# First layer's cross attention: query products of two heads from seven block products each, woven with keys and values in a written order; raw weights in five 4 KB tiles

## The chip, the cores and the metric

The kernel runs on one core of a Trainium2 chip. That core has a matrix engine (PE, with its weight loads shown apart as PEld), a vector engine (DVE), a scalar engine (ACT), GpSimd (POOL) and a queue engine (SP) which issues transfers; each works through its own instructions in the order in which they were recorded, and semaphores tie the engines together. The metric is the device time of one execution in microseconds (us); lower is better.

## What is computed

A trunk of two decoder layers over 512 tokens of width 1024, in float32. Each layer runs a SwiGLU block, a token mixer, a cross attention into 256 memory tokens and a second SwiGLU block, and each step ends in a layer norm of the scaled residual sum. The change concerns the cross attention of layer 0 alone:

```python
def memory_cross_attention(x, mem, wq, wkv, wo):
    B, S, _ = x.shape
    M = mem.shape[1]
    q = (x @ wq).reshape(B, S, XA_HEADS, XA_HEAD_DIM)
    k, v = jnp.split(mem @ wkv, 2, axis=-1)
...
    s = jnp.einsum('bshd,bmhd->bhsm', q, k).astype(jnp.float32) * (XA_HEAD_DIM ** -0.5)
    p = jax.nn.softmax(s, axis=-1).astype(v.dtype)
    o = jnp.einsum('bhsm,bmhd->bshd', p, v).reshape(B, S, D_MODEL)
    return o @ wo
...
        x = layer_norm(a * x + memory_cross_attention(x, mem, xa_wq[i], xa_wkv[i], xa_wo[i]),
                       ln_g[i, 2], ln_b[i, 2])
```

There are 4 heads of width 256; x is 512x1024, wq 1024x1024, wkv 1024x2048.

## The kernel before

Every float32 operand of a matmul is kept as two fp32r parts, a high part (a cast on ACT, L120) and a low part (the difference, on DVE, L121). `mm3` (L205 to L207) forms one product from three matmuls: high by high, low by high, high by low. A weight block of 128x1024 elements is therefore loaded into a tile `raw`, cast on ACT into `wh` and subtracted on DVE into `wl` before PE can use it; there are five buffers each of `wh` and `wl` here, and two of `raw` (8 KB a partition, 1 MB a transfer).

The cross attention of layer 0 follows the differential attention. Its last output product ends in a layer norm for each of the four groups of 128 tokens, `X0` to `X3`: `ln_token` (L366 to L380) on DVE, ACT and POOL, then eight transposes on PE (L489) and four halves of a split, which give the transposed input `xh`, `xl`. Tokens 2 and 3 come late, and `turn_late` puts their transposes behind the first products with the memory, which need no x.

`xa_main` then goes head by head: keys (`xa_k`, result `pk`), values (`xa_v`, `pv`), queries (`xq`). For the queries of a head it takes two blocks of 128 columns of wq, and for each eight `mm3` over 512 tokens. Beside it, `xa_side` yields the heads' attention in six pieces each (scores `xs`, softmax `mx`, `p`, `rx`, transposes `pt`, values `xo`), and `weave` hands out one such piece for every 2500 ns of matmul time that it counts for the main line. `to_tokens` multiplies the outputs `oT` of the first two heads by `xa_wo` while the last heads finish; a second call does the rest and ends in the layer norm of the next step.

The SwiGLU blocks already use seven block products in place of eight (`up`, L681 ff., with `second_factors`, L611 to L644, for the sums of blocks of x). There `more` (L666) adds a further block of weights onto a raw tile in memory by an accumulating transfer, which POOL issues.

The recorded order on an engine is made by a scheduler from the order of the program and its own model of time; the transfers of a queue run in the order in which they were issued.

## Time and profile before

| what | us |
|---|---|
| median of 3 runs | 1932.35 (1931.14 to 1932.38) |
| the profiled execution, its time | 1930.48 |
| the profiled execution, its span | 1928.7 |
| PE busy in it | 1900.9 |
| DVE busy in it | 1564.0 |
| ACT busy in it | 1021.8 |
| POOL busy in it | 315.3 |

The span runs from the first to the last instruction. All times below that begin at some point "of the span" are microseconds from its start. Instructions on one engine overlap a little, so that the distance from start to start is shorter than the duration in a row: two 128x1024 differences that follow each other take 2.35 us, one 1.22 us. The cross attention of layer 0 lies between about 588 and 744 us.

### The profile page before, as it was taken

How to read it: one execution, taken by the hardware profiler on the slowest of the kernel's cores; microseconds unless marked ns; L12 is line 12 of the kernel's file. 1: busy time of each engine (PE TensorE's matmuls, PEld its weight loads, DVE VectorE, ACT ScalarE, POOL GpSimd, SP SyncE). 2: the span in 40 equal slices, each digit the busy share in tenths (PEclk: the TensorE clock that was granted, in tenths of full speed). 3: DMA queues.
4: the chain of work that ended last, by engine and by line, in shares of the span. 5: the costliest groups of instructions: out<-in, count | busy, mean ns of one | idle time of the engine just before them, and what ended most of it. 6: DMA issues, size and time to landing. Idle time of an engine off the chain costs nothing.

```text
span 1928.7 us, 32510 instructions
## 1 busy us (share of the span) xinstructions
PE 1900.9 (99%) x13114; PEld 1740.4 (90%) x13114; DVE 1564.0 (81%) x2200; ACT 1021.8 (53%) x1580; POOL 315.3 (16%) x276
## 2 busy tenths in 40 slices
PE   8999999999999999999999999999999999999998
PEld 8999998888878888999998999999889889999997
DVE  7888889888867558889888988898887568998886
ACT  6555454567755435645554655455445436555553
POOL 2112121111210001211220311212040012111210
PEclk9999999999999999999999999999999999999999
DMA  9978772322124317987785587878244356877861
GB/s 241 217 167 186 169 145 77 91 66 88 64 90 153 110 66 190 182 178 162 144 192 178 106 179 164 181 165 183 85 153 142 110 138 120 180 158 170 183 133 57
DMA packets 246743, 277.96 MB, mean 144 GB/s; under 512 B 8256, under 2 KB 212544, under 8 KB 246592
## 3 DMA queue, kind: packets, MB, share of 16 engines
q0 software_dynamic: 92928, 92.29, 31.3%
q1 hardware_dynamic: 153664, 183.59, 29.7%
q8 instruction: 103, 1.69, 0.4%
q14 instruction: 48, 0.39, 0.1%
HBM read 273.75 MB, written 2.10 MB: 143 GB/s over the span
## 4 chain that ended last, share of the span: by engine, by line
PE 77%; DVE 13%; ACT 3%; DMA 3%; issue 2%; POOL 1%; SPq 1%; DVEq 0%; POOLq 0%; ACTq 0%
PE x L205 6%; PE x L206 6%; PE x L207 6%; PE z L206 4%; PE z L205 4%; PE z L207 4%; PE ps L205 4%; PE ps L207 4%; PE ps L206 4%; DVE wl L121 3%; DMA ra<-in_ffn_w_in_dram 2%; PE px L207 2%; PE px L205 2%; PE px L206 2%; PE y L207 2%
## 5 line engine op out<-in xcount | busy, mean ns | idle before, releaser
L666 POOL DMA_DIRECT2D ra<-in_ffn_w_in_dram x132 | 170.3, 1310 | 990.7 <-DVE wl L121 955.0
L120 ACT CAST wh<-ra 128x1024 fp32r<-128x1024 f32 x184 | 193.7, 1053 | 218.0 <-PE x L206 69.1
L121 DVE TENSOR_TENSOR wl<-ra,wh 128x1024 fp32r<-128x1024 f32 x184 | 223.8, 1220 | 72.0 <-ACT wh L120 71.5
L120 ACT CAST wh<-rc 128x1024 fp32r<-128x1024 f32 x136 | 143.1, 1053 | 118.8 <-PE x L206 43.1
L205 PE MATMUL x<-xe,wh 128*128 128x256 f32 x704 | 195.0, 277 | 0.0
L206 PE MATMUL x<-xe,wh 128*128 128x256 f32 x704 | 194.8, 277 | 0.0
L207 PE MATMUL x<-xe,wl 128*128 128x256 f32 x704 | 194.8, 277 | 0.0
L121 DVE TENSOR_TENSOR wl<-rc,wh 128x1024 fp32r<-128x1024 f32 x136 | 164.7, 1219 | 28.2 <-ACT wh L120 27.9
L120 ACT CAST wh<-b 128x1024 fp32r<-128x1024 f32 x112 | 117.8, 1052 | 131.7 <-PE x L206 67.8
L121 DVE TENSOR_TENSOR wl<-b,wh 128x1024 fp32r<-128x1024 f32 x112 | 136.7, 1221 | 40.2 <-ACT wh L120 40.2
L205 PE MATMUL x<-xh,wh 128*128 128x256 f32 x544 | 151.1, 278 | 0.0
L206 PE MATMUL x<-xl,wh 128*128 128x256 f32 x544 | 150.6, 277 | 0.0
L207 PE MATMUL x<-xh,wl 128*128 128x256 f32 x544 | 150.6, 277 | 0.0
L206 PEld LDWEIGHTS x<-xe,wh 128*128 128x128 f32 x704 | 132.5, 188 | 1.4
L205 PEld LDWEIGHTS x<-xe,wh 128*128 128x128 f32 x704 | 132.1, 188 | 1.3
L207 PEld LDWEIGHTS x<-xe,wl 128*128 128x128 f32 x704 | 132.2, 188 | 0.0
L121 DVE TENSOR_TENSOR wl<-raw,wh 128x1024 fp32r<-128x1024 f32 x64 | 80.3, 1259 | 39.6 <-ACT wh L120 39.1
L206 PEld LDWEIGHTS x<-xl,wh 128*128 128x128 f32 x544 | 102.5, 188 | 0.7
L205 PEld LDWEIGHTS x<-xh,wh 128*128 128x128 f32 x544 | 102.1, 188 | 0.7
L207 PEld LDWEIGHTS x<-xh,wl 128*128 128x128 f32 x544 | 102.2, 188 | 0.0
L207 PE MATMUL y<-xh,wl 128*128 128x256 f32 x352 | 98.6, 280 | 2.1 <-DVE wl L121 0.9
L205 PE MATMUL z<-xh,wh 128*128 128x256 f32 x352 | 97.5, 277 | 0.7 <-ACT xh L120 0.7
(429 smaller groups left out, 6288.9 us busy)
## 6 DMA issues: line engine op xcount, KB each, us to landing
ra<-in_ffn_w_in_dram POOLq DMA_DIRECT2D x132, 512.0 KB, 6.8
rc<-in_ffn_w_in_dram SPq DMA_DIRECT2D x88, 512.0 KB, 5.8
b<-in_ffn_w_out_dram SPq DMA_DIRECT2D x76, 512.0 KB, 4.9
ra<-in_ffn_w_in_dram SPq DMA_DIRECT2D x44, 512.0 KB, 5.3
rc<-in_ffn_w_in_dram POOLq DMA_DIRECT2D x44, 512.0 KB, 7.4
raw<-in_xa_wkv_dram SPq DMA_DIRECT2D x16, 1024.0 KB, 5.5
raw<-in_da_w_qkv_dram SPq DMA_DIRECT2D x16, 512.0 KB, 5.2
raw<-in_xa_wq_dram SPq DMA_DIRECT2D x8, 1024.0 KB, 5.1
```

Of the source, the lines that this page charges most:

```text
L120: self.nc.scalar.copy(hi, src),
L121: self.nc.vector.tensor_sub(lo, src, hi.bitcast(F32)),
L205: mm(out, w[0], x[0], start=start, stop=False, skip_group_check=again)
L206: mm(out, w[0], x[1], start=False, stop=False, skip_group_check=again)
L207: self.last_mm = mm(out, w[1], x[0], start=False, stop=stop, skip_group_check=again)
L666: nc.gpsimd.dma_start(t, source(*block), accum_op=ALU.add)
```

## The change

In layer 0 the queries of heads 0 and 1 (work `a`) and of heads 2 and 3 (work `b`) are each one product of a 512x1024 x with a 1024x512 block of wq, cut into 2x2 blocks and formed from seven block products instead of eight (`query_parts`): 24 matmuls of 256 columns each. The weight operands of products 3, 4 and 2 come from the same raw tile `ra` by accumulating transfers (`more`), each behind the split before it; products 6 and 5 use `rd` in the same way. The blocks of x and their sums (`xa_factors`) take the place of the plain transposed x of tokens 2 and 3. Keys and values are cut into quarters of 512 KB, and one list, `XA_ORDER`, sets the order in which pieces of all these works are recorded. There are now four buffers of `wh` and `wl`, and five raw tiles of 4 KB.

```diff
+XA_ORDER = (
+    "k0 k0 k0 v0 s v0 v0 k1 k1 k1 s v1 v1 v1 "
+    "a a k2 a k2 a v2 a v2 a a A "
+    "b b k2 b b k3 v2 b b k3 b B k3 v3 v3 v3"
+)
...
-        self.ln_next_gb, self.kv_bufs = None, 8
+        self.ln_next_gb, self.kv_bufs, self.raw_rows = None, 8, 4
...
-        got = []
-        for k in range(0, kn, 4):
-            n = min(4, kn - k)
-            raw = self.raw_tile((4, S))
+        got, n = [], self.raw_rows
+        for k in range(0, kn, n):
+            raw = self.raw_tile((n, S))
...
+        self.by_factors = self.ln_next == "ffn" or self.ln_next == "xa" and layer == 0
...
-            o = self.pair("oT")
+            if layer:
+                o = self.pair("oT")
+            else:
+                if c == 0:
+                    both = self.pair("oT" if len(self.oT) < 4 else "xe", (P, 2, S))
+                o = both[0][:, c], both[1][:, c]
             self.split(o[0], o[1], po)
             self.oT.append(o)
...
+    def key_parts(self, w, h, turn=iter(())):
+        ps = self.mm("pk").rearrange("p (c n) -> p c n", c=2)
+        for j in range(2):
+            wk = self.hl([P, KC, P])
+            self.split_weights(wk[0], wk[1], self.raw_quarter(w, 0, h * 256 + j * P, P))
+            for k in range(KC):
+                yield self.mm3(
+                    ps[:, j], (wk[0][:, k], wk[1][:, k]), self.memT[k], k == 0, k == KC - 1
+                )
+            yield None
+        few(turn, 1)
+        kt = self.kv_tiles((P, 2, MEM))
+        self.split(kt[0], kt[1], ps)
+        self.kts.append(kt)
+        yield None
+    def value_parts(self, w, h):
+        ps = self.mm("pv").rearrange("p (m n) -> p m n", m=2)
+        for half in range(2):
+            wv = self.hl([P, 4, MEM])
+            self.split_weights(wv[0], wv[1], self.raw_quarter(w, half * S, D + h * 256, 256))
+            for m in range(2):
+                o = slice(m * P, (m + 1) * P)
+                for k in range(4):
+                    mt = self.memT[half * 4 + k]
+                    yield self.mm3(
+                        ps[:, m], (mt[0][:, o], mt[1][:, o]), (wv[0][:, k], wv[1][:, k]),
+                        half == m == k == 0, half == m == 1 and k == 3, True,
+                    )
+            yield None
+        v = self.kv_tiles((P, 2, MEM))
+        self.split(v[0], v[1], ps)
+        self.kv.append((self.kts[h], v))
+        yield None
+    def xa_factors(self):
+        nc, F, H = self.nc, self.factors, 2 * P
+        a11, a12, a21, s1 = (self.tmp("oT", (P, 4, H)) for i in range(4))
+        def part(i, x, o=slice(0, H)):
+            self.split(F[i][0][:, :, o], F[i][1][:, :, o], x)
+        for t in (2, 3):
+            o = slice(t % 2 * P, (t % 2 + 1) * P)
+            pts = []
+            for half in range(2):
+                pt = self.aux("pt", ("py", "yz")[half]).rearrange("p (c n) -> p c n", c=4)
+                c0 = half * S
+                with self.behind():
+                    self.transpose4(pt, [self.X[t][:, c0 + j * P : c0 + (j + 1) * P] for j in range(4)])
+                pts.append(pt)
+            nc.scalar.copy(a21[:, :, o], pts[0])
+            nc.vector.tensor_tensor(s1[:, :, o], pts[1], a21[:, :, o], ALU.subtract)
+            part(3, s1[:, :, o], o)
+            part(2, pts[1], o)
+            yield
+        for r, (hi, lo) in zip((a11, a12), F):
+            nc.vector.tensor_tensor(r, hi.bitcast(F32), lo.bitcast(F32), ALU.add)
+        s2, s4, s3 = s1, a12, a21
+        nc.vector.scalar_tensor_tensor(s2, s1, -1.0, a11, ALU.mult, ALU.subtract)
+        nc.vector.scalar_tensor_tensor(s4, s2, -1.0, a12, ALU.mult, ALU.subtract)
+        part(6, s4)
+        part(4, s2)
+        nc.vector.tensor_tensor(s3, a11, a21, ALU.subtract)
+        part(5, s3)
+        yield
+    def query_parts(self, w, h, q):
+        nc, H = self.nc, 2 * P
+        def source(row, col):
+            c0 = (h + col - 1) * H
+            return w[(row - 1) * S : row * S, c0 : c0 + H].rearrange("(k p) n -> p k n", p=P)
+        def load(*block):
+            t = self.raw_tile((4, H))
+            nc.sync.dma_start(t, source(*block))
+            return t
+        def more(t, *block):
+            nc.gpsimd.dma_start(t, source(*block), accum_op=ALU.add)
+        def operand(raw):
+            v = self.hl([P, 4, H])
+            self.split(v[0], v[1], raw)
+            return v
+        def product(ps, v, a, start=False):
+            x = self.factors[a]
+            for j in range(2):
+                o = slice(j * P, (j + 1) * P)
+                for k in range(4):
+                    yield self.mm3(
+                        ps[:, j], (v[0][:, k, o], v[1][:, k, o]), (x[0][:, k], x[1][:, k]),
+                        start and j == k == 0, j == 1 and k == 3, True,
+                    )
...
+        def done(i, half, src, by):
+            hi, lo = (t[:, :, halves[half]] for t in q[i])
+            self.split_scaled(hi, lo, src, by)
+        ra, rc = load(1, 1), load(2, 1)
+        x = bank(self.aux("x", "px"))
+        v = operand(ra)
+        more(ra, 1, 2)
+        yield from product(x, v, 0, True)
+        p1 = self.tmp("p", (P, 2, H))
+        nc.scalar.copy(p1, x)
+        yield None
+        y = bank(self.aux("y", "yz"))
+        v = operand(rc)
+        rd = load(2, 2)
+        yield from product(y, v, 1, True)
+        nc.vector.tensor_tensor(p1, y, p1, ALU.add)
+        q[0] = self.pair("q", (P, 2, S))
+        done(0, 0, p1, scale)
+        yield None
+        z = bank(self.aux("z", "yz"))
+        v = operand(ra)
+        more(ra, 2, 2)
+        yield from product(z, v, 3, True)
+        p5 = self.tmp("p", (P, 2, H))
+        nc.scalar.copy(p5, z)
+        yield None
+        v = operand(rd)
+        more(rd, 1, 2)
+        yield from product(z, v, 6)
+        yield None
+        v = operand(ra)
+        more(ra, 2, 1)
+        yield from product(x, v, 4)
+        u2 = self.tmp("p", (P, 2, H))
+        nc.scalar.copy(u2, x)
+        nc.vector.tensor_tensor(u2, z, u2, ALU.add)
+        q[1] = self.pair("q", (P, 2, S))
+        done(1, 0, u2, -scale)
+        yield None
+        yield from product(x, operand(rd), 5)
+        nc.vector.tensor_tensor(p5, x, p5, ALU.add)
+        done(1, 1, p5, -scale)
+        yield None
+        yield from product(x, operand(ra), 2)
+        done(0, 1, x, scale)
+        yield None
+    def xa_woven(self):
+        wq, wkv = self.a["xa_wq"][0], self.a["xa_wkv"][0]
+        self.late, self.kts, second = [], [], self.xa_factors()
+        qs = [[None] * 2 for n in range(2)]
+        works = {n: self.query_parts(wq, 2 * i, qs[i]) for i, n in enumerate("ab")}
+        works["k0"] = self.key_parts(wkv, 0, second)
+        works.update((f"k{h}", self.key_parts(wkv, h)) for h in range(1, XA_H))
+        works.update((f"v{h}", self.value_parts(wkv, h)) for h in range(XA_H))
+        for n in XA_ORDER.split():
+            if n == "s":
+                next(second)
+            elif n in "AB":
+                for q in qs["AB".index(n)]:
+                    self.heads.append((self.clock, [(q[0][:, c], q[1][:, c]) for c in range(2)]))
+            else:
+                for ns in works[n]:
+                    if ns is None:
+                        break
+                    yield ns
+        yield from self.to_tokens(self.oT, self.a["xa_wo"][0], 0, 4, True, False, ALPHA)
...
-    def xa_side(self):
+    def xa_side(self, layer):
         for h in range(XA_H):
-            while h >= len(self.heads) or self.clock < self.heads[h][0] + 3000:
+            while h >= min(len(self.heads), len(self.kv)) or self.clock < self.heads[h][0] + 3000:
                 yield WAIT
-            yield from self.xa_head(*self.heads[h][1])
+            yield from self.xa_head(layer, self.heads[h][1], *self.kv[h])
     def cross_attention(self, layer, ln):
         bufs = dict(q=8, oT=10, gb=2)
         if layer == 0:
-            self.kv, self.keys = [], []
+            self.kv, self.keys, self.raw_rows = [], [], 2
             mem = self.side_pool("mem")
-            with self.other_pools():
-                self.stage["mem"] = mem
-                with self.phase_pool(("gb", "gb"), "p", pT=6, p=4, kv=8, _x=0, **bufs):
-                    self.kvp = self.phase["kv"]
+            with self.stage_pools(4, dict(raw=5), ("wh", "wl", "raw", "kv")):
+                self.stage["mem"], self.kvp = mem, self.stage["kv"]
+                with self.phase_pool(("xe", "xe"), "p", p=4, pT=4, _x=0, xe=6, q=4, oT=4):
...
         else:
             with self.later, self.phase_pool(("gb", "gb"), "p", _x=0, pT=6, p=4, **bufs):
     def xa(self, layer, ln):
         self.heads, self.oT = [], []
-        self.weave(self.xa_main(layer), self.xa_side(), 2500)
+        if layer == 0:
+            self.factors = self.factor_tiles()
+            self.weave(self.xa_woven(), self.xa_side(layer), 1800)
+            pairs = [self.pair("q", (P, 2, S)) for k in range(2)]
+            views = [tuple(t[:, i] for t in pair) for pair in pairs for i in range(2)]
+            first = [lambda v=v: v for v in views]
+        else:
+            self.weave(self.xa_main(layer), self.xa_side(layer), 2500)
+            first = [lambda: self.pair("q")] * 4
         self.begin_ln(layer, ln, 1.0)
...
```

The program up to 588 us of the span keeps its order. From there the rows below show three places; a name's number is that of its tile, `wl` and `wh` are the parts of a weight, `kv` those of a key or value.

The first place is the vector engine while the late tokens' layer norm ends. Before:

```order
L380 SCALAR_TENSOR_TENSOR X3_77<-X3_77,rstd_6651,v_6432 128x1024
L121 TENSOR_TENSOR xl_6441<-pt_6828,xh_6439 128x4x128
L121 TENSOR_TENSOR xl_6442<-pt_6835,xh_6440 128x4x128
L121 TENSOR_TENSOR kv_6827<-pk_6769,kv_6826 128x512
L121 TENSOR_TENSOR xl_6441<-pt_6842,xh_6439 128x4x128
L121 TENSOR_TENSOR xl_6442<-pt_6849,xh_6440 128x4x128
L121 TENSOR_TENSOR wl_6928<-raw_6921,wh_6927 128x1024
L121 TENSOR_TENSOR wl_6993<-raw_6989,wh_6992 128x1024
L121 TENSOR_TENSOR kv_6918<-pv_6868,kv_6917 128x512
L121 TENSOR_TENSOR wl_7021<-raw_6989,wh_7020 128x1024
```

And now, where `oT_6834` to `oT_6837` hold blocks of x and their sums, and `wl_7017` belongs to the first half of the values of head 1:

```order
L128 TENSOR_TENSOR kv_6855<-pk_6773,kv_6854 128x512
L128 TENSOR_TENSOR wl_6971<-raw_6972,wh_6970 128x1024
L1521 TENSOR_TENSOR oT_6837<-pt_6894,oT_6836 128x4x128
L1526 TENSOR_TENSOR oT_6834<-xh_6439,xl_6441 128x1024
L128 TENSOR_TENSOR xl_6442<-oT_6837,xh_6440 128x4x128
L128 TENSOR_TENSOR xl_6442<-pt_6894,xh_6440 128x4x128
L128 TENSOR_TENSOR kv_6936<-pv_6858,kv_6935 128x512
L1526 TENSOR_TENSOR oT_6835<-xh_6439,xl_6441 128x1024
L1528 SCALAR_TENSOR_TENSOR oT_6837<-oT_6837,oT_6834 128x1024
L1532 TENSOR_TENSOR oT_6836<-oT_6834,oT_6836 128x1024
L1529 SCALAR_TENSOR_TENSOR oT_6835<-oT_6837,oT_6835 128x1024
L128 TENSOR_TENSOR wl_7017<-raw_7018,wh_7016 128x1024
```

Between the late tokens' splits (`xl`) and the next weight now stand the sums of x (L1521 to L1532); the weights `wl_6928` and `wl_6993` were three and four rows behind `kv_6827`, while `wl_7017` is eleven behind `kv_6855`.

The second place is the matrix engine where it takes up that weight; `x_7084` is the first product of `a`, `pk_7152` the keys of head 2. Before, the queries of head 0 follow the values of head 0:

```order
L206 MATMUL pv_6868<-wl_6865,mem6h_6763 128x256
L207 MATMUL pv_6868<-wh_6864,mem6l_6764 128x256
L205 MATMUL xq_6931<-xh_6439,wh_6923 128x512 [waits DVE_49,Activation_49]
L206 MATMUL xq_6931<-xl_6441,wh_6923 128x512 [waits DVE_49]
L207 MATMUL xq_6931<-xh_6439,wl_6924 128x512
```

And now, after the keys of head 1, and a little further on, inside the values of head 1:

```order
L214 MATMUL pk_6939<-mem6h_6763,wl_6971 128x256
L212 MATMUL pv_7015<-wh_7016,mem0h_6736 128x256 [waits DVE_49]
L212 MATMUL x_7084<-xh_6439,wh_7085 128x256 [waits Activation_49]
L213 MATMUL x_7084<-xl_6441,wh_7085 128x256
L212 MATMUL y_7116<-xh_6439,wh_7117 128x256 [waits Activation_49]
L213 MATMUL y_7116<-xl_6441,wh_7117 128x256
L213 MATMUL pv_7015<-wl_7017,mem0h_6736 128x256 [waits DVE_49]
```

```order
L213 MATMUL pv_7015<-wl_7017,mem2h_6745 128x256
L214 MATMUL pv_7015<-wh_7016,mem2l_6746 128x256
L212 MATMUL pv_7015<-wh_7046,mem4h_6754 128x256
L212 MATMUL pk_7152<-mem0h_6736,wh_7153 128x256 [waits DVE_49,Activation_49]
L213 MATMUL pk_7152<-mem0l_6737,wh_7153 128x256
L213 MATMUL pv_7015<-wl_7047,mem4h_6754 128x256 [waits DVE_49]
```

Single matmuls of other works are recorded ahead of the weight that the value product needs: two each of `x_7084` and `y_7116`, and two of `pk_7152`, whose weight `wh_7153` is loaded after `wl_7017` has read its raw tile.

The third place is the scalar engine between the third and the fourth block product of `a`. Before there is no transfer that adds onto a tile here:

```order
L125 ACTIVATE q_6981<-xq_6931 128x512 [waits PE_49]
L120 CAST wh_7085<-raw_7079 128x1024 [waits DVE_49]
L120 CAST wh_7176<-raw_7174 128x1024 [waits DVE_49,DMAHW3_49,PE_49,Activation_49]
L125 ACTIVATE q_6985<-xq_6932 128x512 [waits PE_49]
L120 CAST wh_7180<-raw_7174 128x1024 [waits DVE_49,PE_49]
```

And now, where `raw_7080` is `ra`, `p_7213` is the copy of the third product, and the fourth is added onto its bank `z_7183`:

```order
L127 CAST wh_7245<-raw_7121 128x1024 [waits DVE_49,DMAHW6_49,PE_49,Activation_49]
L132 ACTIVATE q_7148<-p_7114 128x2x256 [waits DVE_49]
L127 CAST wh_7275<-raw_7277 128x1024 [waits DMAHW1_49,PE_49,Activation_49]
L127 CAST wh_7305<-raw_7080 128x1024 [waits DMASW5_49,PE_49,Activation_49]
L1598 COPY p_7213<-z_7183 128x512 [waits PE_49]
L127 CAST wh_7341<-raw_7343 128x1024 [waits DMAHW2_49,PE_49,Activation_49]
```

The copy `p_7213` that frees the bank stands behind `wh_7305`, which waits for the second accumulating transfer onto `raw_7080`.

In `b` the vector engine has such a place too: `kv_7555` empties the bank of `pk_7152`, which `pk_7648` (keys of head 3) needs next, and stands behind `wl_7693`, which waits for the second accumulating transfer of `b`:

```order
L1417 TENSOR_SCALAR p_7502<-p_7502,rx_7500 128x256 x2
L1589 TENSOR_TENSOR p_7466<-y_7468,p_7466 128x512
L128 TENSOR_TENSOR wl_7693<-raw_7432,wh_7692 128x1024
L1409 TENSOR_REDUCE mx_7539<-xs_7526 128x2
L133 SCALAR_TENSOR_TENSOR q_7551<-p_7466,q_7550 128x2x256
L128 TENSOR_TENSOR kv_7555<-pk_7152,kv_7554 128x512
L1415 RECIPROCAL rx_7541<-sm_7540 128x2
L128 TENSOR_TENSOR pT_7482<-pt_7579,pT_7481 128x256
L1417 TENSOR_SCALAR p_7543<-p_7543,rx_7541 128x256 x2
```

Before, no row in this stage's vector queue waits for a transfer that was started by another row of the same queue through POOL.

28 lines of the change are left out of this document (18 added, 10 removed).

## The prediction

> **What bounds the kernel now.** I read the page first.
>
> ```profile
> PE 1900.9 (99%) x13114; PEld 1740.4 (90%) x13114; DVE 1564.0 (81%) x2200; ACT 1021.8 (53%) x1580; POOL 315.3 (16%) x276
> PE 77%; DVE 13%; ACT 3%; DMA 3%; issue 2%; POOL 1%; SPq 1%; DVEq 0%; POOLq 0%; ACTq 0%
> ```
>
> PE is busy nearly all the time, and the chain that ended last runs over it. Whether that holds in this stage, the windows of the stage say (us; busy time of PE, PEld, DVE, ACT, POOL; granted clock; DMA).
>
> ```profile
> 588.60:617.00 28.40, 27.41 (x189) 24.82 (x188) 21.50 (x27) 13.79 (x22) 0.60 (x1) 1.00 0.64 204
> 617.00:650.00 33.00, 33.00 (x231) 30.26 (x230) 17.34 (x27) 15.19 (x27) 0.00 (x0) 1.00 0.33 101
> 650.00:680.00 30.00, 30.00 (x204) 27.24 (x203) 16.84 (x27) 13.08 (x26) 0.00 (x0) 1.00 0.38 128
> 712.00:744.00 32.00, 31.62 (x142) 25.56 (x141) 18.51 (x34) 10.24 (x20) 4.53 (x4) 1.00 0.58 168
> ```
>
> PE stands still for only 1.37 us of the stage (28.40-27.41 and 32.00-31.62). So the change can gain what it takes off PE and hardly more, and any new wait of PE, which works in order, is paid in full. DVE has slack on average, but 21.50 of the first 28.40 us are taken.
>
> The timeline of PE gives the paces (start, duration, line, tiles, count).
>
> ```profile
> 595.38 1.03 PE L489 MATMUL pt<-ident,X 128*128 128x128 f32 x8
> 596.17 0.36 PE L205 MATMUL pv<-wh,mem0h 128*128 128x256 f32 x1
> 600.10 0.28 PE L205 MATMUL pv<-wh,mem0h 128*128 128x256 f32 x1
> 602.57 0.28 PE L205 MATMUL pv<-wh,mem6h 128*128 128x256 f32 x1
> 602.92 0.39 PE L205 MATMUL xq<-xh,wh 128*128 128x512 f32 x1
> 614.12 0.28 PE L205 MATMUL pk<-mem0h,wh 128*128 128x256 f32 x1
> 616.85 0.28 PE L205 MATMUL pk<-mem0h,wh 128*128 128x256 f32 x1
> L205 PE MATMUL xq<-xh,wh 128*128 128x512 f32 x64 | 25.8, 403 | 0.0
> ```
>
> **The saving.** One head's queries are 48 matmuls of 512 columns and last 614.12-602.92 = 11.20 us; the group's row has 64 first matmuls, so 192 in all and four heads: 44.8 us. Now there are 14 block products of 24 matmuls of 256 columns. A key half has the same form: 616.85-614.12 = 2.73 us. 14 x 2.73 = 38.2, saving **6.6 us**. All other matmuls and transposes keep number and size. A value half of 24 runs at (602.57-600.10)/7 x 8 = 2.82; at that pace the saving would be 5.3.
>
> **The vector queue behind the late tokens.** Rows of DVE now, and the durations of the kinds that are added (they exist in the SwiGLU blocks; first the timeline, then groups by form):
>
> ```profile
> 592.18 1.22 DVE L121 TENSOR_TENSOR wl<-raw,wh 128x1024 fp32r<-128x1024 f32 x1
> 594.84 1.29 DVE L378 SCALAR_TENSOR_TENSOR X<-X,mean,v 128x1024 f32<-128x1024 f32 x1 [0.18 <-ACT rt L374]
> 598.38 1.28 DVE L121 TENSOR_TENSOR xl<-pt,xh 128x512 fp32r<-128x512 f32 x2
> 601.37 2.35 DVE L121 TENSOR_TENSOR wl<-raw,wh 128x1024 fp32r<-128x1024 f32 x2
> 609.26 1.23 DVE L121 TENSOR_TENSOR wl<-raw,wh 128x1024 fp32r<-128x1024 f32 x1 [3.70 <-ACT wh L120]
> L631 DVE TENSOR_TENSOR hb<-pt,hb 128x512 f32<-128x512 f32 x8 | 5.4, 681 | 0.0
> L611 DVE TENSOR_TENSOR hb<-xh,xl 128x1024 f32<-128x1024 f32 x8 | 9.7, 1214 | 0.0
> L637 DVE SCALAR_TENSOR_TENSOR sr<-hb 128x1024 f32<-128x1024 f32 x1 | 1.2, 1211 | 0.0
> L121 DVE TENSOR_TENSOR xe<-hb,xe 128x1024 fp32r<-128x1024 f32 x2 | 2.4, 1212 | 0.0
> ```
>
> From start to start a 1024 wide one takes 1.14 (2.35-1.22, rounded), a layer norm's 1.20, a 512 wide one 0.60. Both programs agree up to 592.18. From there DVE now has, up to `wl_7017`: ten 1024 wide (five weights, two sums, `s2`, `s3`, `s4`), two of the layer norm, eight 512 wide, a short mean and about 0.3 us of waiting: 11.4+2.4+4.8+0.1+0.3 = 19.0, done at **611.3**. About 7 us of it are the new sums; before, DVE had nothing left at 605.6 (609.26 less the 3.70 us of waiting in its row).
>
> PE: first value half from 596.17 to 599.0, eight transposes of X3 (596.17-595.38 = 0.8, held to 599.1 by the layer norm) to 599.9, second value half to 602.7, the two key halves of head 1 (5.46) to **608.2**. The five matmuls recorded early take 0.6; `wl_7017` is needed at 608.8 and there at 611.4: **wait 2.6** (1.6 to 3.5 if the queue runs 1 us better or worse).
>
> The second half of these values needs `wl_7047`: behind `wl_7017` come a key eviction, three `xe` and itself, 0.6+4x1.14, so 616.5. PE has done its first half at 614.2. But the two `pk_7152` matmuls recorded there need `wh_7153`, whose transfer starts when `wl_7017` has read its raw tile, and then a cast:
>
> ```profile
> raw<-in_da_w_qkv_dram SPq DMA_DIRECT2D x16, 512.0 KB, 5.2
> L120 ACT CAST wh<-raw 128x1024 fp32r<-128x1024 f32 x26 | 27.1, 1051 | 25.7 <-PE xq L206 11.7 <-PE pk L206 8.9 <-DMA raw<-in_xa_wkv_dram 5.1
> ```
>
> 611.4+5.2+1.05 = 617.7: **wait 3.5**; 2.2 if only `wl_7047` counts, 4.5 with a transfer 1 us slower.
>
> **The accumulating transfers.** Their price, from the start of POOL's instruction to landing, is on the page and, for single ones, in the issues of short windows:
>
> ```profile
> ra<-in_ffn_w_in_dram POOLq DMA_DIRECT2D x132, 512.0 KB, 6.8
> ra<-in_ffn_w_in_dram POOLq DMA_DIRECT2D x1, 512.0 KB, 5.9
> L718 ACT COPY sp<-x 128x512 f32<-128x512 f32 x1 | 0.6, 565 | 0.0
> ```
>
> Each starts only behind the split (`wl`) before it, so from one `wl` to the next pass 5.9 to 6.8, a cast of 1.05 and 1.14: 8.1 to 9.0. In `a`, `wl_7086` ends at 617.7; `wl_7185` then at 625.8 to 626.7, the second transfer lands at 631.7 to 633.5, `wh_7305` is cast, and only then the copy that frees the bank of the third product: 633.4 to 635.2. PE gets there at 617.8 + 0.2 + 2.7 + three times 2.5 (two matmuls of each are done) + two times 2.73 = 633.7: **wait 1.0** (0 to 1.7).
>
> In `b` the second accumulating weight, `wl_7693`, stands in the queue ahead of `kv_7555`, which frees a bank for the keys of head 3. From the end of the fourth product of `a` (which frees a weight buffer) the chain takes 2.5 for hand-over, cast and split, twice 8.1 to 9.0, and 1.8 for three 512 wide rows: 20.5 to 22.3 us. PE has in that time 168 matmuls of 256 columns (19.1) and four transposes (0.4), 19.5. Wait 1.0 to 2.8, 2.0 taken; behind it the transposes of `p_7543` wait for a reciprocal, a split and two scalings in the same queue, about 1 us more. Together **3.0** (1.0 to 3.9).
>
> **Smaller ones**: a bank of `a` read late (0.3), softmax rows behind weights in `b` (0.7 and 0.3): **1.2** (0 to 2.5). The other added work, six more weight splits, six copies and six additions, finds cover: after 650 DVE is busy about 17 of 30 us, ACT 13. The gains of the next layer norm now load late, into `xe` tiles that the products of `b` free; the first output product (96 matmuls of 512 columns, 22.4 us at 11.20/48) covers them, and without that cover the 5 us of a load are paid. POOL's transfers for the next block stand ahead of its `rstd` as before.
>
> Sum: -6.6+2.6+3.5+1.0+3.0+1.2 = **+4.7 us** against the profiled execution's 1930.48 (span 1928.7), so 1935.2; its time is 1.87 under the median of the runs shown, and 1932.35+4.7 = **1937.0**. With all waits at their low ends (4.8) it is -1.8, with all at their high ends (16.1) and the smaller saving +10.8; a middling case of this kind lies at -0.5 to +9.5.
>
> The Trainium skill, "DMA: Bandwidth & Descriptors", section "Anatomy of one DMA — SWDGE (gpsimd) path", fits a GpSimd transfer by 2.0 us plus its bytes over 436 thousand per us; 512 KB would take 3.2 us, and with POOL's instruction an estimate of 4.5. By that the two waits on accumulating transfers would vanish and the sum be near +1. The rows say 5.9 and 6.8, so I go by them.
>
> **Rivals.**
> - *Only the vector queue's waits count.* For it: the two of them are fixed by counted rows, while the others hang on transfers that land within 2 us of their need. Against it: the copy and the eviction stand behind those transfers in order. -6.6+2.6+2.2 = -1.8: 1930.5.
> - *Faster.* The vector queue is the place: were DVE through with `wl_7017` by 609.3, so that its waits cost 2 in all and the transfers cost nothing, 1932.35-6.6+2 = 1927.8. Decisive is whether all waits together stay under 2.8. For it: the prices of the added rows are from other stages, and ACT is less busy here. Against it, DVE has hardly a gap to make up 2 us in:
>
> ```profile
> 580.00:600.00 20.00, 18.70 (x138) 16.86 (x137) 19.82 (x29) 13.36 (x24) 1.54 (x2) 1.00 0.46 158
> ```
>
> - *The clock falls in the waits.* At the start PE runs at half pace after standing still:
>
> ```profile
> 4.21 1.94 PE L489 MATMUL pt<-ident,X 128*128 128x128 f32 x8 [4.21 <-DMA X<-in_x_dram]
> 8.21 1.97 PE L489 MATMUL pt<-ident,X 128*128 128x128 f32 x8 [2.06 <-DMA X<-in_x_dram]
> 10.19 0.41 PE L681 MATMUL x<-xl,wh 128*128 128x256 f32 x1
> 11.47 0.41 PE L681 MATMUL x<-xl,wh 128*128 128x256 f32 x1
> 12.00 0.28 PE L681 MATMUL x<-xh,wh 128*128 128x256 f32 x1
> ```
>
>   From 8.21 to about 11.7 it works at half pace (from 10.19 to 11.47 six steps of 0.21), which loses 1.75 us. Two waits of 2.6 and 3.5 close together could bring one such fall: 1938.8. The Trainium skill, "TensorE: Matmul & The Clock Gate", section "Part 1: The HAM clock gate (the "warmup" mystery)", makes the clock half after an idle window of about 3.4 us and full after a busy one as long. The start agrees with it; whether a wait of 3.5 us fills such a window no run here shows.
> - *A late tail.* Heads 2 and 3 are scored only after `B`, and their softmax, the gains and the last weights crowd into the 22 us of the first output product; 4 us of new waits there give 1941.
> - That the change doesn't do what it says I leave out: the recorded order has the 336 matmuls in place of 192.
>
> **How the numbers follow.** Forecast 0.52, only the queue 0.13, faster 0.15, clock 0.12, tail 0.08. About 0.2%, 3.9 us, is what a measurement of this kernel can tell from no change. Slower: 0.36 of the forecast (its part above +3.9), clock and tail, 0.56. Same: 0.16 of the forecast and 0.10 of the queue's case, 0.26. Faster: 0.15 and 0.03, 0.18. The forecast's own range is 1931.8 to 1941.9; to leave out no more than 2 in 10 it reaches down into the faster case: 1928.0 to 1942.5.
>
> **What would show it.** PE's waits in this stage would rise from 1.4 to some 13 us: at about 608 and 614 for `pv` on `wl`, near 634 at the bank `z` for ACT's copy, and near 664 at `pk` for `kv`. The query products should take 2.73 us each. The prediction is wrong if PE works through there without waits (then 1926), if the products run slower than 2.8, or if the waits sit in the output products.

## The result, and the profile after

| | before | changed |
|---|---|---|
| median of 4 runs each, us | 1932.37 (1931.14 to 1933.86) | 1946.12 (1942.59 to 1947.56) |
| the profiled execution, its time | 1930.48 | 1946.07 |
| its span | 1928.7 | 1944.3 |

The changed kernel is slower: the ratio is 1.0068, with a 95% interval of 1.0056 to 1.0080, some 13 us. The prediction said 1937.0, in a range of 1928.0 to 1942.5; the direction was right, the size was not, and the time lies outside the range.

The page of the changed kernel, the rows of engines and of the chain:

```profile
PE 1906.6 (98%) x13258; PEld 1751.5 (90%) x13258; DVE 1584.7 (82%) x2222; ACT 1034.6 (53%) x1597; POOL 327.6 (17%) x284
PE 74%; DVE 15%; ACT 4%; DMA 3%; issue 2%; POOL 1%; SPq 0%; DVEq 0%; POOLq 0%; ACTq 0%
```

PE's share of the chain fell from 77 to 74%, DVE's and ACT's rose. The windows of the stage (columns as before: PE, PEld, DVE, ACT, POOL, granted clock, DMA share, GB/s):

```profile
588.60:617.00 28.40, 24.97 (x195) 23.56 (x193) 28.36 (x35) 18.14 (x27) 0.95 (x1) 0.94 0.36 112
617.00:650.00 33.00, 28.16 (x208) 27.56 (x209) 14.03 (x14) 10.49 (x13) 5.22 (x4) 0.90 0.79 172
650.00:680.00 30.00, 28.86 (x234) 27.67 (x233) 20.44 (x30) 16.21 (x30) 5.12 (x4) 1.00 0.72 151
680.00:712.00 32.00, 31.98 (x241) 30.15 (x240) 23.44 (x39) 19.25 (x41) 0.00 (x0) 1.00 0.44 143
```

Three things are to be seen. PE stands still for 3.43, 4.84 and 1.14 us in the first three windows, where it stood still for 0.99, 0 and 0 us before. The vector engine is full in the first window (28.36 of 28.40). And the granted clock, 1.00 everywhere before, is 0.94 and 0.90: 0.06 x 28.4 + 0.10 x 33 = 5.0 us of PE's time. The view of PE's waits in this stage says at what (waiting matmul, what released it; us in total, times, longest):

```profile
PE z L212 <- ACT p L1598: 2.4, 1, 2.4
PE pv L213 <- DVE wl L128: 1.1, 1, 1.1
PE z L212 <- ACT wh L127: 1.0, 1, 1.0
PE pk L212 <- ACT wh L127: 0.9, 1, 0.9
PE z L214 <- DVE wl L128: 0.8, 1, 0.8
PE y L212 <- ACT wh L127: 0.7, 1, 0.7
PE z L212 <- DVE p L1589: 0.5, 1, 0.5
```

They stand where the prediction put them, at the values of head 1 (`pv` on `wl`), at `pk` behind them, and at the bank `z` of the third and fourth product, which waits for ACT's copy `p` of line 1598. But those at `z` are 1.0, 0.8 and 2.4 us, in place of 1.0 in all. The timeline of PE shows what follows a wait (start, duration):

```profile
612.25 0.39 PE L213 MATMUL pv<-wl,mem0h 128*128 128x256 f32 x1 [1.13 <-DVE wl L128]
613.30 0.28 PE L212 MATMUL pv<-wh,mem2h 128*128 128x256 f32 x1
613.42 0.28 PE L213 MATMUL pv<-wl,mem2h 128*128 128x256 f32 x1
...
640.26 0.39 PE L212 MATMUL z<-xe,wh 128*128 128x256 f32 x1 [2.43 <-ACT p L1598]
641.01 0.42 PE L214 MATMUL z<-xe,wl 128*128 128x256 f32 x1
641.22 0.42 PE L212 MATMUL z<-xe,wh 128*128 128x256 f32 x1
```

From start to start 0.12 us at 613.3, but 0.21 at 641.0: soon after PE stood still, its matmuls go at half pace for some 3 us. That happens three times in this profile, from 613.7, from 630.6 and from 640.8 us (in run 12, a second profile, not at the third product).

The stage can be measured by itself, from POOL's fourth `rstd` of the step ahead to the fourth of its own; the next block from there to the next `rstd`. In the timeline of POOL, before and then the changed kernel:

```profile
595.93 0.60 POOL L376 TENSOR_TENSOR rstd<-var,mhalf 128x1 f32<-128x1 f32 x1 [9.79 <-ACT var L375]
758.69 0.72 POOL L376 TENSOR_TENSOR rstd<-var,mhalf 128x1 f32<-128x1 f32 x1 [5.48 <-ACT var L375]
1058.86 1.36 POOL L376 TENSOR_TENSOR rstd<-var,mhalf 128x1 f32<-128x1 f32 x1 [46.88 <-ACT var L375]
```

```profile
596.39 0.95 POOL L384 TENSOR_TENSOR rstd<-var,mhalf 128x1 f32<-128x1 f32 x1 [9.11 <-ACT var L383]
768.41 1.01 POOL L384 TENSOR_TENSOR rstd<-var,mhalf 128x1 f32<-128x1 f32 x1 [4.89 <-ACT var L383]
1073.18 1.36 POOL L384 TENSOR_TENSOR rstd<-var,mhalf 128x1 f32<-128x1 f32 x1 [46.91 <-ACT var L383]
```

The stage took 162.76 us and takes 172.02 (+9.3); the next SwiGLU block, whose code is the same, took 300.17 and takes 304.77 (+4.6). Of the second the prediction has no word. There the weights `rc` come late. The tile's rows say when they are cast (duration min/median/max in ns, first and last start), before and after; the third row is from the waits of SP's queue in the changed kernel:

```profile
L120 ACT CAST wh<-rc x9: 1043/1055/1062, 740.3 to 793.6; 128x1024 fp32r<-128x1024 f32 x9
```

```profile
L127 ACT CAST wh<-rc x6: 1038/1047/1049, 768.2 to 790.4; 128x1024 fp32r<-128x1024 f32 x6
...
SPq L670 <- PE ps L214: 23.3, 1, 23.3
```

A load of `rc` stands in SP's queue for 23.3 us until the last output product `ps` is done: the new layout puts `rc` where the last output weights lie (`kv`). The casts begin at 768 in place of 740 and fall on the late tokens' work; the third product's weight is late by 1.0 us.

### The profile page after: what moved, and what is told of

It reads as the page before. It is cut to its first block, busy times and chain, and to the rows that moved or that the text cites. A ratio compares the mean times of both kernels' runs of the same rounds, so it can differ in the third digit from the quotient of the medians.

```text
span 1944.3 us, 32901 instructions
## 1 busy us (share of the span) xinstructions
PE 1906.6 (98%) x13258; PEld 1751.5 (90%) x13258; DVE 1584.7 (82%) x2222; ACT 1034.6 (53%) x1597; POOL 327.6 (17%) x284
## 4 chain that ended last, share of the span: by engine, by line
PE 74%; DVE 15%; ACT 4%; DMA 3%; issue 2%; POOL 1%; SPq 0%; DVEq 0%; POOLq 0%; ACTq 0%
PE x L212 7%; PE x L213 7%; PE x L214 7%; PE z L212 4%; PE z L213 4%; PE z L214 4%; PE ps L212 4%; PE ps L214 4%; PE ps L213 4%; DVE wl L128 3%; PE px L212 2%; PE px L214 2%; PE px L213 2%; PE y L214 2%; PE pz L214 1%
## 5 line engine op out<-in xcount | busy, mean ns | idle before, releaser
L127 ACT CAST wh<-rc 128x1024 fp32r<-128x1024 f32 x136 | 143.0, 1053 | 116.5 <-PE x L213 43.3
L212 PE MATMUL x<-xe,wh 128*128 128x256 f32 x736 | 204.4, 278 | 0.0
L213 PE MATMUL x<-xe,wh 128*128 128x256 f32 x736 | 204.0, 277 | 0.0
L214 PE MATMUL x<-xe,wl 128*128 128x256 f32 x736 | 204.0, 277 | 0.0
L212 PE MATMUL x<-xh,wh 128*128 128x256 f32 x576 | 160.2, 278 | 0.0
L213 PE MATMUL x<-xl,wh 128*128 128x256 f32 x576 | 159.6, 277 | 0.0
L214 PE MATMUL x<-xh,wl 128*128 128x256 f32 x576 | 159.5, 277 | 0.0
L213 PEld LDWEIGHTS x<-xe,wh 128*128 128x128 f32 x736 | 138.7, 188 | 1.4
L212 PEld LDWEIGHTS x<-xe,wh 128*128 128x128 f32 x736 | 138.2, 188 | 1.6 <-ACT p L1608 0.2
L214 PEld LDWEIGHTS x<-xe,wl 128*128 128x128 f32 x736 | 138.2, 188 | 0.0
L128 DVE TENSOR_TENSOR wl<-raw,wh 128x1024 fp32r<-128x1024 f32 x70 | 86.7, 1245 | 42.7 <-ACT wh L127 42.0
L213 PEld LDWEIGHTS x<-xl,wh 128*128 128x128 f32 x576 | 108.6, 189 | 0.8
L127 ACT CAST wh<-raw 128x1024 fp32r<-128x1024 f32 x70 | 72.8, 1049 | 65.1 <-DMA raw<-in_xa_wq_dram 23.6
```

The costliest lines, as they stand in the source:

```text
L127: self.nc.scalar.copy(hi, src),
L128: self.nc.vector.tensor_sub(lo, src, hi.bitcast(F32)),
L212: mm(out, w[0], x[0], start=start, stop=False, skip_group_check=again)
L213: mm(out, w[0], x[1], start=False, stop=False, skip_group_check=again)
L214: self.last_mm = mm(out, w[1], x[0], start=False, stop=stop, skip_group_check=again)
```

## The experiments

All are compared with the kernel before on the same chip. Stage and next block are lengths of the profiled execution, from `rstd` to `rstd` as above; what lies ahead of the stage differed by up to 5 us between executions and isn't in them. "Again" is one execution each (runs 11 and 12).

| kernel | median | ratio to before (95%) | stage | next block |
|---|---|---|---|---|
| before; again | 1932.37; 1930.38 | | 162.76; 162.76 | 300.17; 300.08 |
| changed; again | 1946.12; 1942.60 | 1.0068 (1.0056 to 1.0080) | 172.02; 171.33 | 304.77; 303.34 |
| 1 sums of x later | 1937.50 | 1.0027 (1.0016 to 1.0038) | 162.60 | 304.75 |
| 2 places exchanged | 1943.34 | 1.0058 (1.0043 to 1.0073) | 171.38 | 301.16 |
| 3 plain transfers | 1935.01 | 1.0020 (1.0011 to 1.0030) | 162.71 | 303.06 |
| 4 waits filled | 1944.53 | 1.0069 (1.0052 to 1.0086) | 171.50 | 303.06 |
| 5 = 1 and 2 | 1934.58 | 1.0014 (1.0006 to 1.0023) | 164.18 | 301.16 |
| 6 = 5, results first | 1936.36 | 1.0022 (1.0012 to 1.0031) | 167.64 | 301.34 |
| 7 = 6, plain transfers | 1928.15 | 0.9983 (0.9973 to 0.9992) | 157.68 | 301.15 |
| 8 = 5, vector sums | 1929.11 | 0.9985 (0.9976 to 0.9994) | 158.89 | 302.86 |
| 9 = 6, vector sums | 1929.14 | 0.9984 (0.9975 to 0.9993) | 158.61 | 301.16 |
| 10 = changed, vector sums | 1934.27 | 1.0013 (1.0003 to 1.0022) | 161.68 | 303.17 |

**1. The sums of x later.**

```diff
-    "k0 k0 k0 v0 s v0 v0 k1 k1 k1 s v1 v1 v1 "
-    "a a k2 a k2 a v2 a v2 a a A "
+    "k0 k0 k0 v0 s v0 v0 k1 k1 k1 v1 v1 v1 "
+    "a a s k2 a k2 a v2 a v2 a a A "
```

> The piece of the order that forms the sums of x moves from between the keys and values of head 1 to behind the first two products of a. Theory (vector queue): the waits of PE at 610 to 618 us (0.7+1.1+0.9) vanish with the half-pace stretch behind them (1.3); the first accumulating transfer starts about 8 us earlier, so that the waits at bank z (1.05+0.76+2.43) and their two half-pace stretches (3.4) shrink as well: 1935 to 1939. Rival (an accumulating transfer takes 8 to 9 us wherever it starts and the chain of three sets the end): only the first group goes, 1942. Rival (the sums are merely late elsewhere): a new wait at the fourth product, 1946 or more.

1937.5, as the theory had it. No wait is left at 610 to 618 us, and the granted clock doesn't fall in the stage. PE's waits from 600 to 700 us:

```profile
PE z L212 <- DVE p L1589: 1.2, 1, 1.2
PE x L212 <- DVE p L1614: 1.1, 1, 1.1
PE z L212 <- ACT p L1598: 0.7, 1, 0.7
```

The fourth product begins at 632.38, which is 33.5 us after the fourth `rstd` (598.92); in the changed kernel it was 640.26 - 596.39 = 43.9. The 10.4 us between them cover the 9.4 by which the stage is shorter. The first accumulating transfer starts at 612.87, 14.0 us after that `rstd`, where it was 619.01 - 596.39 = 22.6. It lands sooner too, and so does the second one onto the same tile, as the issues of two short windows here say (around 612.87 and 624.80; in the changed kernel it was 9.2 and 7.7, shown under run 3):

```profile
raw<-in_xa_wq_dram POOLq DMA_DIRECT2D x1, 512.0 KB, 5.8
...
raw<-in_xa_wq_dram POOLq DMA_DIRECT2D x1, 512.0 KB, 5.9
```

So this edit moves two things, the start of the transfers and the time that they take.

**2. The places exchanged.** `oT`, free after the first output product, comes to lie where `rc` will be, and `kv` in its place:

```diff
-            with self.stage_pools(4, dict(raw=5), ("wh", "wl", "raw", "kv")):
-                self.stage["mem"], self.kvp = mem, self.stage["kv"]
-                with self.phase_pool(("xe", "xe"), "p", p=4, pT=4, _x=0, xe=6, q=4, oT=4):
+            with self.stage_pools(4, dict(raw=5), ("wh", "wl", "raw")):
+                self.stage["mem"] = mem
+                with self.phase_pool(("xe", "xe"), "p", oT=4, p=4, pT=4, _x=0, xe=6, q=4, kv=8):
+                    self.kvp = self.phase["kv"]
```

> Only the places in memory of kv and oT are exchanged in this stage, so that the tiles rc of the next block lie under a tile that is free after the first output product. PE's order does not change. Theory: the next block loses 3.8 us because its rc weights land after 764 us (a wait of 1.2 us, then a slower pace of its matmuls); with rc loaded by about 745 they are back: 1942. Rival (the pace there is chance, or comes from the stage before): 1946.

The next block is down to 301.16, and PE waits for nothing there up to 800 us, where it waited for 1.0 and 0.2 us; the stage stays at 171.38. The medians alone (1.0058 and 1.0068, with intervals that overlap) wouldn't tell this; the length of the block does. The tile's row, with the first cast at 746.5:

```profile
L127 ACT CAST wh<-rc x8: 1044/1054/1056, 746.5 to 799.9; 128x1024 fp32r<-128x1024 f32 x8
```

**3. Plain transfers**, which leave the sums of weight blocks out (there are four of these transfers in `a` and four in `b`, of each four, three go onto `ra`):

```diff
-            nc.gpsimd.dma_start(t, source(*block), accum_op=ALU.add)
+            nc.gpsimd.dma_start(t, source(*block))
```

> The three accumulating transfers of each pair of heads become plain ones that overwrite their tile, from the same queue at the same place; the sums of weight blocks are left out of the computation. Theory A (the price of accumulating sets the waits at bank z): landing falls from 6 to 9 us to about 5, the waits at z (4.2 us) go to 1 or less with their half-pace stretches (3.4): 1938 to 1940. Theory B (they start late and share the queues with other loads): landing changes by 1 us or less, 1943 to 1946.

1935.0, better than theory A asked. The issues of two short windows (610 to 624 and 624 to 632 us; KB each, median us from issue to landing), in the changed kernel and then here:

```profile
raw<-in_xa_wkv_dram SPq DMA_DIRECT2D x4, 512.0 KB, 4.8
raw<-in_xa_wq_dram POOLq DMA_DIRECT2D x1, 512.0 KB, 9.2
...
raw<-in_xa_wq_dram POOLq DMA_DIRECT2D x1, 512.0 KB, 7.7
```

```profile
raw<-in_xa_wkv_dram SPq DMA_DIRECT2D x4, 512.0 KB, 5.0
raw<-in_xa_wq_dram POOLq DMA_DIRECT2D x1, 512.0 KB, 5.6
...
raw<-in_xa_wq_dram POOLq DMA_DIRECT2D x2, 512.0 KB, 4.7
```

The two accumulating transfers that PE's waits hang on land 9.2 and 7.7 us after their issue; plain ones, beside the same loads of SP, 5.6 and 4.1 (4.7 is the median of this one and the one onto `rd`, 5.4). No wait is left at `z`, while those at 610 to 617 us and their half pace are all still there. So it is the chain of accumulating transfers that costs the changed kernel these 9.3 us. That the early waits cost nothing doesn't follow: run 7, which has plain transfers and no early waits, has a stage 5.0 us shorter still, and its other edits are worth less than 1 us where nothing waits for a transfer or nothing else is changed (runs 9 and 2).

**4. The waits filled.**

```diff
+        def idle(n):
+            ps, m = self.aux("d", "py"), self.memT[0][0]
+            for i in range(n):
+                with self.behind():
+                    mm = nc.tensor.matmul(ps[:, :MEM], m[:, :P], m, start=i == 0, stop=i == n - 1)
+                self.last_mm = mm
...
         more(ra, 2, 2)
+        if h == 0:
+            idle(8)
...
         more(rd, 1, 2)
+        if h == 0:
+            idle(20)
```

> 8 and 20 matmuls of 256 columns with no use (0.9 and 2.3 us) are put ahead of the third and the fourth product of a, where PE waits 1.05 and 2.43 us; all else keeps its order. Theory (PE's pace halves because it stood still): the half-pace stretches at 631 and 640 us vanish and about 3.4 us are saved though the work is more: 1942 to 1944. Rival (the half pace has another cause, such as the transfers or the form of the matmuls): both stretches stay, 1946 to 1947.

Neither side was right as a whole. The windows around the third and the fourth product, in the changed kernel and then here, where the axis is about 1.2 us earlier:

```profile
628.00:636.00 8.00, 6.19 (x37) 5.79 (x37) 5.92 (x6) 4.98 (x6) 2.56 (x2) 0.79 0.43 73
638.00:646.00 8.00, 5.74 (x35) 5.74 (x36) 2.56 (x3) 3.53 (x4) 1.29 (x1) 0.79 0.91 177
```

```profile
627.00:635.00 8.00, 8.00 (x70) 8.00 (x70) 5.92 (x6) 4.01 (x6) 2.56 (x2) 1.00 0.61 109
637.00:645.00 8.00, 7.39 (x65) 7.19 (x64) 3.67 (x3) 3.42 (x4) 1.29 (x1) 1.00 0.83 174
```

With matmuls in the place of the waits the granted clock stays at 1.00: the half pace comes from standing still, the cause that the theory named. The fourth product carries this, since half pace followed its wait in both profiles of the changed kernel (2.43 and 4.40 us); the third went without it in run 12 with nothing filled in. And where nothing is filled in here, it comes back: behind a wait of 2.24 us at `pk` (616.35) PE goes at half pace from 616.8 to 620.0. But the stage takes 171.5 us, as before the edit, and the ratio is the same. The fourth product begins 43.3 us after the `rstd` (638.47 - 595.15). PE gained its pace and waited for the transfers instead.

**5. Both edits, 1 and 2.**

> Both edits together: the sums of x behind the first two products of a, and the places of kv and oT exchanged. Theory (two separate losses, 9.4 us in the stage and 3.6 to 4.6 us in the next block, of which the first edit takes back the one and the second the other): 1.5 to 2 us above the kernel before at most, ratio 1.0000 to 1.0012. Rival (the next block's loss comes from what the stage leaves behind in the clock or the pace of PE): the second edit adds nothing, ratio 1.0027 as with the sums alone.

1.0014, a little above the range given. The next block is down to 301.16, as the theory said; the stage took 1.6 us more than in run 1, with a wait of 1.2 us for ACT's copy of the fifth product in place of 0.3.

**6. Results first**, on top of 5:

```diff
-        z = bank(self.aux("z", "yz"))
+        z = bank(self.aux("z", "py"))
...
-        nc.scalar.copy(p5, z)
+        held = nc.scalar.copy(p5, z)
...
-        v = operand(ra)
+        v = operand(ra, held)
         more(ra, 2, 1)
...
-        v = operand(rc)
+        v = operand(rc, None, self.added)
...
-        nc.vector.tensor_tensor(p5, x, p5, ALU.add)
+        self.added = nc.vector.tensor_tensor(p5, x, p5, ALU.add)
```

where `operand` now records its cast behind the first and its difference behind the second of these instructions.

> On top of the last one: three results of products are taken out of their banks ahead of a weight split that waits for a transfer (the copy of the third product ahead of the cast for the fifth, the sum of the sixth ahead of a split of b), and the third product gets its bank from py, so that in b it no longer shares one with the second product. Theory (the waits of PE that are left, 0.73, 1.13 and 1.20 us in the run with the sums later, are results that stand behind such splits): 2 to 3 us less than the last one, ratio 0.9985 to 0.9997, so faster than before by up to 3 us. Rival (the splits moved back make their own products late): no better than the last one.

The theory fell: 1.0022, a stage of 167.6. The three waits that were named are gone or down to 0.3 us, but another result now stands behind casts that wait for transfers, the copy of the fifth product, in `a` and again in `b`. PE's waits, and ACT's timeline with that copy:

```profile
PE x L212 <- ACT p L1611: 5.4, 2, 3.5
...
PE z L212 <- ACT p L1601: 0.3, 1, 0.3
```

```profile
640.47 1.99 ACT L1557 CAST wh<-raw 128x1024 fp32r<-128x1024 f32 x2 [4.19 <-DMA raw<-in_xa_wq_dram]
642.37 0.58 ACT L1611 COPY p<-x 128x512 f32<-128x512 f32 x1
```

**7. The same with plain transfers** (the edit of run 3, with the same sums left out).

> The last one with plain transfers that overwrite in place of the accumulating ones; the sums of weight blocks are left out of the computation. Theory (with the sums later, the accumulating transfers have time enough): within 1.5 us of the last one. Rival (the accumulating transfers still set the pace of a and b): 3 us or more below it.

Some 8 us below run 6, so the rival was right: even with the sums of x later, the accumulating transfers set the pace of `a` and `b`. Without them the stage is 5.1 us shorter than before.

**8, 9, 10. The sums of weight blocks by the vector engine**, a complete form. Run 8 on top of 5, run 9 on top of 6, run 10 on the changed kernel alone:

```diff
         def more(t, *block):
-            nc.gpsimd.dma_start(t, source(*block), accum_op=ALU.add)
+            b = block[0] if len(block) == 1 else load(*block)
+            nc.vector.tensor_tensor(t, t, b, ALU.add)
...
-        more(ra, 2, 2)
+        more(ra, rd)
```

> On top of the run with the sums of x later and the places exchanged: the sums of weight blocks are no longer made by accumulating transfers but by the vector engine, from blocks that are loaded plainly ahead of time (in one case from a block that is there anyway); the computation is complete. Theory (the accumulating transfer, 5.6 to 9.4 us between one split and the next, still holds a and b back, the vector engine has the 9 us for eight more additions): the waits at the results (1 us each) shrink, ratio 0.9980 to 0.9995, faster than before. Rival (the additions make the vector queue late): ratio 1.0010 or more.

> The same with the results taken out first and the third product's bank from py, so it is the valid form of the run with plain transfers, which stood at ratio 0.9983. Theory: 0.9980 to 0.9990, and 1 to 2 us below the one without the results first. Rival (the additions cost what the transfers cost): 1.0010 or more.

> The changed kernel with this one edit alone: sums of weight blocks by the vector engine in place of accumulating transfers; the sums of x stay where they were, as do the places in memory. Theory (a late start and a slow transfer make the stage's loss together, so that either alone takes back most of it): 5 to 9 us below the changed kernel, ratio 1.0020 to 1.0045, with the waits at 610 to 617 us still there. Rival (the vector queue at 600 to 617 us is the cause, more work on it makes it worse): 1946 or more.

Runs 8 and 9 stand at 0.9985 and 0.9984, with intervals below 1: they beat both kernels, by some 3 us against the one before. Results first adds nothing once no transfer is waited for, against the 1 to 2 us that the theory of run 9 gave it. In run 8 the longer of PE's two waits from 600 to 700 us, and the row of the additions among the vector engine's groups:

```profile
PE pk L212 <- DVE kv L128: 0.5, 1, 0.5
...
L1553 DVE TENSOR_TENSOR raw<-raw 128x1024 f32<-128x1024 f32 x8 | 9.7, 1217 | 0.0
```

Eight additions of 1.2 us, and no wait above half a microsecond. Run 10 takes back 10.3 us of the changed kernel's stage by this edit alone, though its waits at 609 to 616 us are longer in sum (0.7, 0.9 and 2.0 in place of 0.7, 1.1 and 0.9): more work on the full vector queue, and yet a stage 1.1 us shorter than in the kernel before. Its ratio, 1.0013, is better than the range of its theory.

Runs 2, 5, 8 and 10 together part the two causes. Run 8 has neither an early sum of x nor an accumulating transfer, and its stage takes 158.89 us. The early sums alone cost 2.8 us more (run 10), the accumulating transfers alone 5.3 (run 5; 9.0 in the order of runs 6 and 9), both together 12.5 (run 2): 4.4 us come only with both. (Run 10 has the places not exchanged; that alone moved the stage by 0.6 us or less.)

**11, 12. Both kernels again**, unchanged, for a second profile.

> The kernel before once more, for a second profile. The stage (from the fourth rstd of the step ahead to the fourth of its own) took 162.8 us, the next block 300.2 and the token mixer's norm in layer 1 33.0, against 172.0, 304.8 and 34.1 in the changed kernel. Theory: the stage repeats within 0.3 us; the next block repeats within 0.3 where its matmuls find the quicker pace, and is 1.7 to 2 us longer where they don't. Whether the 1.1 us in layer 1 belong to the change or to chance is open: if they are chance, this run shows 33.8 to 34.2 at least here or in the changed kernel's second profile a value near 33.

> The changed kernel once more, for a second profile. Theory: the stage takes 171.3 to 172.1 us, the next block 303 to 305, with the wait of about 1 us for the third product's weight. Rival (what was read as the change's cost in the next block is chance): a next block of 301 or less.

The stage repeats (162.76, and 171.33 against 172.02), and so does the cost in the next block: 303.34 against 300.08. So 1.4 us of the next block's 4.6 in the first profile don't repeat. With the places not exchanged, the six profiles of changed forms have 303.06 to 304.77 there; with them exchanged, five have 301.15 to 301.34 and run 8 has 302.86, without a wait of PE. The 1.1 us in layer 1 (34.1 and 34.1 from `rstd` to `rstd` in the changed kernel, 33.0 and 32.9 before) are not chance (the other changed forms have 33.8 to 34.2); they lie in two differences on DVE whose order hasn't changed. The rows of the tile `pw`, before and changed:

```profile
L121 DVE TENSOR_TENSOR wl<-pw,wh x2: 1210/1448/1687, 1433.5 to 1435.2; 128x1024 fp32r<-128x1024 f32 x2
```

```profile
L128 DVE TENSOR_TENSOR wl<-pw,wh x2: 1687/1992/2298, 1447.9 to 1449.5; 128x1024 fp32r<-128x1024 f32 x2
```

Why they are slower wasn't tried and stays open.

## Why the prediction was too low

- **What bounds it.** Right: what PE waits in this stage and cannot make up is paid. Run 4 adds a limit: PE's own speed ahead of a wait is worth nothing where the wait's end is set by a transfer. PE stood still for 9.4 us from 588.6 to 712, where the prediction had some 13 in the stage, and lost about 5 more at half pace.
- **The saving, 6.6 us.** Right in kind: where PE isn't held, a product of 24 takes 2.72 us (in run 8 the third one from 623.14 to 625.86). At the slower of two paces (last section) one took 2.83, as the fifth of `a` in the changed kernel did (647.55 to 650.38), the price that the prediction named as its other one. Less of it was had over the whole stage: run 7, with no wait of `z`, is 5.1 us shorter than before, the complete forms 8 and 9 are 3.9 and 4.2. From `rstd` to `rstd` PE was busy for 161.8 us before and for 158.1 in run 8, where it waits for 0.8: 3.7 less. Where the rest of the 6.6 went was not traced.
- **First and second wait, 2.6 and 3.5 us.** The queue of the vector engine was worked out rightly: `wl_7017` was predicted for 611.3 and ended at about 612.2 (the matmul that waits for it starts at 612.25) on an axis that is 1.15 us later, the shift of the first key matmuls. But PE came later than assumed, since it waited 0.7 for `y`'s cast and then lost its pace, so the two waits were 1.1 and 0.9. They aren't free, as run 10 beside run 8 shows (2.8 us); but in the changed kernel PE stands behind them at `z` for the end of a transfer, which an earlier PE doesn't move (run 4).
- **Third wait, 1.0 us: the step that failed.** The prediction let each accumulating transfer land 5.9 to 6.8 us after its issue and so put PE's arrival and the copy's end within 2 us of each other. The first one started when the prediction said (617.7; 619.01 on the axis that is 1.15 us later). But the two landed after 9.2 and 7.7 (8.0 and 8.0 in run 12), and the copy was done 3.9 to 5.7 us later than predicted: the fourth product, which waits for it, starts at 640.26, or 639.1 on the prediction's axis, in place of 633.4 to 635.2. The waits at `z` were 1.05, 0.76 and 2.43 us, and the half pace after them lies in the same delay: the fourth product began 10.4 us later than in run 1. The price came from rows of the SwiGLU blocks; the kernel before has no such transfer in this stage. It held in run 1 (5.8 and 5.9), where the transfers start early, and failed for the late start. SP loaded four quarters of `wkv` in the window of the slowest, but in run 1 the first one landed after 5.8 us with three such loads in its window, so what stretches them was not isolated. Runs 3 and 10 change the transfers alone and take back 9.3 and 10.3 us of the stage; run 1 starts them 8.6 us earlier and takes back 9.4. Of the 12.5 us that the late start and the accumulating transfers cost together, 2.8 and 5.3 come with one of them alone and 4.4 only with both.
- **Fourth wait, 3.0, and smaller ones, 1.2.** 0.5, 0.3 and 0.2 us were measured there (`z` on `p`, `pt` on `p`, `pk` on `kv`): the chain of `b` fitted. In run 1, where PE gets there 9.7 us earlier after the `rstd`, they are 1.2, 0.3 and 0.3.
- **Left out of the sum: the next block**, 3.2 to 4.6 us. The prediction looked at the gains and at POOL's queue behind the stage, not at what the new layout of memory puts where the next block's weights are to be loaded. Run 2 shows it: with the places exchanged the two waits there (1.2 us) are gone, and the block takes 301.16, 2.2 to 3.6 us less. About 1 us over the kernel before is left and stays open, and so does the pace of PE's matmuls, which was slow in run 8 without a wait (302.86). The 1.1 us in layer 1 were left out too.
- **The rivals.** "Only the vector queue's waits" and "faster" are out. In the clock's case the mechanism was right, three falls in place of one (two in run 12), but at `z` its price was not paid (run 4). And the prediction said that no run shows what a wait of 3.5 us does, but the timeline of the kernel before has a wait of 3.11 us with half pace behind it, 0.21 us from start to start:

```profile
1435.28 0.58 PE L206 MATMUL ps<-wl,pooled 128*128 128x256 f32 x1 [3.11 <-DVE wl L121]
...
1435.88 0.41 PE L205 MATMUL ps<-wh,pooled 128*128 128x256 f32 x1
1436.09 0.41 PE L206 MATMUL ps<-wl,pooled 128*128 128x256 f32 x1
```

  The late tail didn't come: PE is busy for all but 0.02 us from 680 to 712.

The sum with what was measured: 8.6 to 9.3 us in the stage in place of 4.7, 3.2 to 4.6 in the next block and 1.1 in layer 1 in place of nothing, 12.9 to 15.0 together, against 13.8 between the medians (some 13 by the ratio).

## What to carry to other kernels

Where steps hang on each other through a transfer, price the transfer by the slow rows as well as by the median, and follow the whole chain, since a late start and slow links together can cost more than the two alone (here 12.5 us against 2.8 and 5.3). When a stage's memory is laid out anew, look which tiles of the next stage come to lie on its last ones: that stage's first loads wait for them. And a saving on the bounding engine is had only when the feeding chain keeps up: here it came once the sums were made on an engine with room, from blocks loaded ahead.

## What was not expected of the hardware

- Waits well under 3 us can bring half pace. 1.05 and 0.76 us within two did (from 630.6), and in run 6 a single wait of 1.89:

```profile
679.64 0.39 PE L212 MATMUL x<-xe,wh 128*128 128x256 f32 x1 [1.89 <-ACT p L1611]
...
681.24 0.41 PE L213 MATMUL x<-xe,wh 128*128 128x256 f32 x1
681.45 0.41 PE L214 MATMUL x<-xe,wl 128*128 128x256 f32 x1
```

  while in run 10 waits of 0.94 and 2.04 us, 5 us apart, brought none. The length of the waits doesn't settle it: 0.70 and 0.94 us, 1.4 us apart, stand at the same place of run 3, where half pace follows from 612.6 us, and of run 10, where none follows. The Trainium skill, "TensorE: Matmul & The Clock Gate", section "Part 1: The HAM clock gate (the "warmup" mystery)", asks for an idle window of about 3.4 us; these waits are shorter, and the measurement decides.
- An accumulating transfer of 512 KB took between 5.6 and 10.0 us from issue to landing in this stage (10.0 in run 6). The Trainium skill, "DMA: Bandwidth & Descriptors", section "Anatomy of one DMA — SWDGE (gpsimd) path", gave the estimate of 4.5 us in the prediction; the plain ones of run 3 (3.8 to 5.6) come near it, the accumulating ones don't.
- The same matmuls of 256 columns run at one of two paces at a granted clock of 1.00, and stay at it for tens of microseconds. The same 30 us of the axis in the next block (which stands 2.1 us earlier in the second), in the changed kernel's first and in its second profile (PE's busy time and, in brackets, its matmuls):

```profile
790.00:820.00 30.00, 30.00 (x257) 30.00 (x256) 21.83 (x24) 15.87 (x19) 8.41 (x7) 1.00 1.19 229
```

```profile
790.00:820.00 30.00, 30.00 (x267) 30.00 (x266) 20.97 (x23) 15.18 (x19) 7.79 (x6) 1.00 1.13 222
```

  257 and 267 matmuls, 0.117 and 0.112 us each. It changes at a wait or where one form of matmul follows another; what sets it was not found.
